# A SwiGLU feed-forward whose gate-and-up product is cut into halves: eight products of halves against seven

## The chip, the core and the metric

One core of a Trainium2 chip runs the whole program. The metric is the device time of one execution in microseconds (us). Five engines take part: TensorE (PE in the profile, with its weight loads as PEld), VectorE (DVE), ScalarE (ACT), GpSimd (POOL) and SyncE (SP), which here only issues transfers.

## The reference, cut to what matters

The program computes two layers of a decoder trunk on 512 tokens of 1024 features. Each layer adds to the residual `x` a first feed-forward, a token mixer (pooling, attention, a state-space branch called S5) and a second feed-forward, each read through an RMS norm that is scaled and shifted by vectors made from a conditioning vector `c` (the reference calls this adaLN):

```python
mod = (jax.nn.silu(c) @ ada_w + ada_b).reshape(B, N_MOD, D_MODEL)   # nine vectors per layer
h = _modulate(_rms_norm(x, norm_ffn1), sh1, sc1)
x = x + 0.5 * g1[:, None, :] * _swiglu(h, ffn1_w_in, ffn1_w_out)

def _swiglu(h, w_in, w_out):              # w_in (1024, 5632), w_out (2816, 1024)
    gate, up = jnp.split(h @ w_in, 2, axis=-1)
    return (jax.nn.silu(gate) * up) @ w_out
```

Everything is float32.

## The kernel before, in words

**Names.** A feed-forward is called by layer and place: (0,1), (0,2), (1,1), (1,2). Its 2816 hidden features are 22 blocks `f` of 128. The 22 are worked through in `CHUNKS` of 6, 6, 6 and 4.

**Matmuls.** A float32 operand is kept as two parts, `hi` (rounded to the type fp32r, by ScalarE) and `lo` (the rest, by VectorE). `mm3` makes one product of three matmuls: hi by hi, hi by lo, lo by hi. For one block `f`, `glu_mm` does 8 slices of 128 features, gate and up, three matmuls each: 48 matmuls of 512 columns (one for each token). `glu_post` then applies SiLU, multiplies gate and up and splits the result. After a chunk its blocks are multiplied by `w_out` and `x_update` (VectorE, L417) adds them to `x`: for a chunk of 6 that is 144 matmuls of 512 columns. In the last chunk, of 4 blocks, `out_halves` does this for each half of the tokens apart, in 192 matmuls of 256 columns, so that the norm of the next stage (`norm_half`) can begin with the finished half. The first two blocks of a feed-forward are likewise done in halves of 256 columns as the norm delivers them, feature slice by feature slice (all but the very first feed-forward).

**Weights.** They come as one stream of units of 512 KB in the order of `stream_plan`. `loader` fetches a unit into one of two raw buffers, `splitter` makes its `hi` (ScalarE, L404, 128x1024) and `lo` (VectorE, L413, 128x1024) into one of four slots of each kind, and the matmuls that have used a unit give its slots back (`done`). Gate and up take two units per block `f`, `w_out` one unit per block.

**Other work beside the matmuls.** `ada_task` streams `ada_w` in pieces of 512 KB and multiplies each by SiLU(c) on VectorE (L417, 128x1024): seven vectors of layer 0 (56 pieces) in the feed-forward (0,1), nine vectors of layer 1 (72 pieces) in (0,2). `s5_build` prepares tables for the mixer, in (0,1) and in (1,1), much of it on GpSimd (L440).

**The order of the work.** There is no hand-written order. The kernel runs a small event simulation in the host program (`Sched`), with a cost for each instruction, and issues each instruction on its engine in the order in which the simulation reaches it. On the chip each engine keeps that order and waits on semaphores. So a costed order is fixed before the run, and an engine that is later than the simulation thought holds up what is queued behind it.

**Lines of helpers.** Every operation goes through a helper, so the profile names these lines: L404 ScalarE, L413 and L417 VectorE (two tensors; two tensors and a scalar), L440 GpSimd (two tensors), L453 matmul, L469 transpose, L546 DMA issue on SP.

Of the kernel before, what the change touches and what calls it, by code (L numbers as in the profile page):

```python
# [89 lines left out]

def wide_block(l, w):

    return FIRST_BLOCK if (l, w) == (0, 1) else 2


def stream_plan():

    plan = []
    for l in range(DEPTH):
        for w in (1, 2):  # L100
            if w == 2:
                for k4 in range(2):
                    plan += [("cv", l, k4), ("ka", l, k4)]
# [9 lines left out]
            f0 = 0  # L113
            for n in CHUNKS:
# [16 lines left out]
def pack_stream(inp):  # L131
# [240 lines left out]
def kernel(ctx, tc, xT, c, ada, ws, sp, mp, bc, w1, c_cols, ada_pe, cst, out):  # L372
# [79 lines left out]
    def mm(o, l, r, start=True, stop=True):  # L452
        nc.tensor.matmul(o, l, r, start=start, stop=stop)  # L453
# [80 lines left out]
    raws = Slots(K, ["r0", "r1"])  # L534
# [16 lines left out]
    def loader():  # L551
        for i, u in enumerate(plan):
# [3 lines left out]
            rn = yield from raws.get()  # L556
            r = sbt([128, 1024], F32, rn)
# [3 lines left out]

    def splitter():
        for i, u in enumerate(plan):
            yield dmax[i]
            d = units[i]
            n = unit_cols(u)
            hn = yield from his.get()
            hi = sbt([128, 1024], F32R, hn)[:, :n]
            t = pts(hi, d["raw"], 1.0, 1.0) if u[0] in POOL_HI else act(hi, d["raw"])
            ln = yield from los.get()  # L570
            lo = sbt([128, 1024], F32R, ln)[:, :n]
            yield t
            t = (ptt if i in POOL_LO or u[0] in POOL_LOK else tt)(lo, d["raw"], f(hi), OP.subtract)
            raws.put(d["rn"], t)
            d.update(hn=hn, ln=ln, hi=hi, lo=lo)
            K.set(d["ev"], t)
# [22 lines left out]
    def ada_task(l, ms, slots, scr, pace, after):  # L599
# [14 lines left out]
        for i, (m, j) in enumerate(todo):  # L614
# [5 lines left out]
            t = stt(scr, slots[:, i % depth, :], 1.0, silu_c["c"], OP.mult, OP.mult,  # L620
# [85 lines left out]


# [109 lines left out]
    def out_halves(ufo, ah, al, aev, gcol, nxt, Rs):  # L817
# [7 lines left out]
        for half in nxt["order"]:  # L825
            for dg in range(2):
                wide = Rs is None and half == nxt["order"][0] and dg == 0
                for dis in ((0, 1, 2, 3),) if wide else ((0,), (1,), (2,), (3,)):
# [18 lines left out]
    def final_store(st):  # L847
        for half in range(2):
# [160 lines left out]
    def mixer(l, st, nxt, s5):  # L1009
# [734 lines left out]
        def attention():  # L1744
# [10 lines left out]
            yield all_p  # L1755
            K.set(nxt["gate"])
# [236 lines left out]
    def main():  # L1993
# [11 lines left out]
        for l in range(DEPTH):  # L2005
            s5 = dict(ev=Ev(), rot_ev=Ev(), room=Ev())
            K.spawn(s5_rot(s5))
            if l > 0:
                s5.update(alloc_s5())
                Kreg = sbt([128, 4096], F32, "K")  # L2010
                Vreg = sbt([128, 2048], F32, "V")
# [8 lines left out]
            else:  # L2020
                K.spawn(s5_build(l, s5, Kreg, Vreg))
            nx = new_norm(l, 1)
            for half in range(2):
                K.spawn(norm_half(nx, half))
            yield from ffn(l, 1, st, nx, s5["room"])
# [9 lines left out]
            if l + 1 < DEPTH:  # L2035
                Kreg = sbt([128, 4096], F32, "K")
                Qreg = sbt([128, 4, D], F32, "Q")
                K.spawn(ada_task1(Qreg, Kreg))
                nx = new_norm(l + 1, 0)
                for half in range(2):  # L2040
                    K.spawn(norm_half(nx, half))
            else:
                nx = new_norm(l, 0)
                K.spawn(final_store(nx))
            yield from ffn(l, 2, st, nx)
# [6 lines left out]
    def ada_task0(Qreg, Kreg):  # L2052
# [3 lines left out]
        yield from ada_task(0, [2, 3, 4, 5, 6, 7, 8], Qreg, scr, 2500, mod_ev)  # L2056
        K.set(ada_done[0])

    def ada_task1(Qreg, Kreg):
        yield K.now + 30000  # L2060
        yield from load_c(Kreg)
        yield from ada_task(1, list(range(9)), Qreg, Kreg[:, 1024:2048], 2500, mod_ev)
# [52 lines left out]
```

## Time and profile before

| what | us |
|---|---|
| median of 3 runs | 2084.37 |
| lowest and highest run | 2080.19, 2084.98 |
| the profiled execution: its time | 2086.14 |
| the profiled execution: span from first to last instruction | 2084.3 |
| busy in the span: TensorE | 2030.9 |
| VectorE | 1222.0 |
| ScalarE | 722.3 |
| GpSimd | 555.0 |

The profiled execution took 1.8 us more than the span of its instructions and also 1.8 us more than the median of the runs. A busy share is an average over stages that have different limits; what a change in a stage is worth is read from that stage.

### The profile page before, as it was taken

The page shows a single profiled execution, that of the slowest core. Times are in us where ns is not written, and L with a number is a line of the kernel's source. Part 1 is how long each engine was busy: PE and PEld are TensorE (multiplying, and loading weights), DVE is VectorE, ACT ScalarE, POOL GpSimd, SP SyncE. Part 2 cuts the span into 40 slices and gives each one's busy share as a digit, 9 for nine tenths or more (in the row PEclk, how much of TensorE's full clock was granted, in tenths as well). Part 3 has the DMA queues.
Part 4 walks back from the last instruction along what each step waited for, and adds up shares of the span by engine and source line. Part 5 has one row for each costly group of instructions (what it writes and reads, how often), then busy time and mean ns, then how long its engine had stood idle before and what let it go on. Part 6 is the DMA issues. An engine that isn't in the chain of part 4 may idle for free.

```text
span 2084.3 us, 27503 instructions
## 1 busy us (share of the span) xinstructions
PE 2030.9 (97%) x10538; PEld 1710.6 (82%) x10538; DVE 1222.0 (59%) x2165; ACT 722.3 (35%) x1262; POOL 555.0 (27%) x813
## 2 busy tenths in 40 slices
PE   5999999999999999999999999999999999999999
PEld 4788888897988888888898888889888888888888
DVE  6779743477876777774364334336678774333333
ACT  4423222343665522222242222224237644222221
POOL 4039102545735200000024400063466360000000
PEclk9999999999999999999999999999999999999999
DMA  6668722231200387773323222222211012222222
GB/s 244 250 212 286 247 91 92 79 111 49 67 21 22 117 276 254 262 263 130 97 86 111 91 91 91 91 91 101 81 44 61 1 61 101 91 92 98 95 91 82
DMA packets 71124, 251.34 MB, mean 121 GB/s; under 512 B 8016, under 2 KB 10448, under 8 KB 70480
## 3 DMA queue, kind: packets, MB, share of 16 engines
q1 hardware_dynamic: 70992, 249.58, 35.6%
q8 instruction: 83, 1.36, 0.3%
q14 instruction: 49, 0.40, 0.1%
HBM read 247.45 MB, written 2.10 MB: 120 GB/s over the span
## 4 chain that ended last, share of the span: by engine, by line
PE 85%; DVE 7%; POOL 3%; ACT 2%; issue 2%; DMA 0%; SPq 0%; DVEq 0%; POOLq 0%; ACTq 0%
PE p L453 83%; DVE s L413 3%; POOL s L440 3%; PE p L469 3%; DVE s L417 2%; ACT s L404 2%; DVE s L1274 1%; DVE s L422 0%; DVE p L1567 0%; DMA s<-in_x_dram 0%; DVE s L432 0%; POOL s L449 0%; ACT L404 0%; DVE s L1567 0%; DVE s L424 0%
## 5 line engine op out<-in xcount | busy, mean ns | idle before, releaser
L453 PE MATMUL p<-s,s 128*128 128x512 f32 (+5 forms) x9862 | 1978.2, 360 | 41.8 <-DVE s L413 21.1
L453 PEld LDWEIGHTS p<-s,s 128*128 128x128 f32 (+1 forms) x9862 | 1635.0, 193 | 348.7 <-DVE s L413 23.4
L413 DVE TENSOR_TENSOR s<-s,s 128x1024 fp32r<-128x1024 f32 (+7 forms) x558 | 516.7, 947 | 460.6 <-ACT s L404 450.2
L404 ACT ACTIVATE s<-s 128x1024 fp32r<-128x1024 f32 (+4 forms) x576 | 451.4, 806 | 756.5 <-PE p L453 587.9
L440 POOL TENSOR_TENSOR s<-s,s 128x256 f32<-128x256 f32 (+13 forms) x363 | 287.4, 811 | 242.7 <-DVE s L424 116.5
L404 ACT ACTIVATE s<-p 128x512 f32<-128x512 f32 (+9 forms) x325 | 162.8, 524 | 477.6 <-PE p L453 398.0
L440 POOL TENSOR_TENSOR s<-s 128x256 f32<-128x256 f32 (+4 forms) x244 | 165.3, 683 | 545.7 <-ACT s L404 402.7
L413 DVE TENSOR_TENSOR s<-s,p 128x512 f32<-128x512 f32 x89 | 60.9, 686 | 217.9 <-PE p L453 206.0
L417 DVE SCALAR_TENSOR_TENSOR s<-s,s 128x1024 f32<-128x1024 f32 (+1 forms) x143 | 182.0, 1276 | 1.8 <-DMA s<-in_ada_dram 0.3
L417 DVE SCALAR_TENSOR_TENSOR s<-p,s,s 128x512 f32<-128x512 f32 (+2 forms) x210 | 128.8, 620 | 68.6 <-PE p L453 67.4
L413 DVE TENSOR_TENSOR s<-p,s 128x512 fp32r<-128x512 f32 (+8 forms) x205 | 109.7, 556 | 52.4 <-ACT s L404 38.5
L469 PE MATMUL p<-s,s 128*128 128x128 f32 (+1 forms) x548 | 82.5, 278 | 8.2 <-DVE s L413 7.4
L469 PEld LDWEIGHTS p<-s,s 128*128 128x128 f32 (+1 forms) x548 | 66.6, 142 | 21.1 <-DVE s L413 7.7
L404 ACT ACTIVATE s<-p,s 128x512 f32<-128x512 f32 (+3 forms) x132 | 69.5, 533 | 30.1 <-DVE s L1567 22.3
L449 POOL TENSOR_SCALAR s<-s,s 128x512 f32<-128x512 f32 (+3 forms) x128 | 68.9, 560 | 24.1 <-DVE s L413 22.9
L449 POOL TENSOR_SCALAR s<-s 128x128 f32<-128x128 f32 (+9 forms) x58 | 34.0, 604 | 136.7 <-PE p L453 113.8
L1567 DVE CUSTOM_DVE_ANT_0 p<-p,s 128x512 f32<-128x512 f32 (+3 forms) x128 | 61.3, 500 | 9.7 <-PE p L453 9.5
L1809 POOL MEMSET s<- 128x8 f32 x2 | 0.2, 111 | 213.6 <-PE p L453 213.6
L404 ACT ACTIVATE s<-s,s 128x256 fp32r<-128x256 f32 x80 | 40.1, 507 | 47.1 <-DVE s L417 47.0
L417 DVE SCALAR_TENSOR_TENSOR s<-s,s,s 128x256 fp32r<-128x256 f32 (+2 forms) x100 | 49.1, 502 | 1.7 <-ACT s L404 1.5
L417 DVE SCALAR_TENSOR_TENSOR s<-s,s,p 128x256 f32<-128x256 f32 (+1 forms) x88 | 43.3, 502 | 6.8 <-PE p L453 5.2
L404 ACT ACTIVATION_READ_ACCUMULATOR s<-p,s 128x1 f32 x128 | 26.0, 203 | 0.0
(36 smaller groups left out, 204.2 us busy)
## 6 DMA issues: line engine op xcount, KB each, us to landing
s<-in_ws_dram SPq DMA_DIRECT2D x304, 512.0 KB, 3.5
s<-in_ada_dram SPq DMA_DIRECT2D x143, 512.0 KB, 5.2
s<-in_w_dram SPq DMA_DIRECT2D x4, 1024.0 KB, 6.3
s<-in_x_dram SPq DMA_DIRECT2D x8, 256.0 KB, 6.2
out_dram<-s SPq DMA_DIRECT2D x16, 128.0 KB, 1.7
s<-in_ws_dram SPq DMA_DIRECT2D x4, 420.0 KB, 3.2
s<-in_c_dram SPq DMA_DIRECT2D x2, 512.0 KB, 5.1
s<-in_bc_dram SPq DMA_DIRECT2D x2, 512.0 KB, 5.7
```

The costliest lines, as they stand in the source:

```text
L404: nc.scalar.activation(o, i, func, **kw)
L413: nc.vector.tensor_tensor(o, a, b, op)
L417: nc.vector.scalar_tensor_tensor(o, a, s, b, op0=op0, op1=op1, **kw)
L440: nc.gpsimd.tensor_tensor(o, a, b, op)
L449: nc.gpsimd.tensor_scalar(o, a, s1, s2, op0=op0, op1=op1)
L453: nc.tensor.matmul(o, l, r, start=start, stop=stop)
L469: nc.tensor.transpose(o, i, idn)
L1274: nc.vector.tensor_tensor_scan(zz, keep[:, 2, 4 * q + j:4 * q + j + 1].to_broadcast([128, 128]), zz, 0.0, op0=OP.mult, op1=OP.add)
L1567: nc.vector.tensor_tensor_reduce(b[:, :L], b[:, :L], mask, -0.125, 3.0e38, OP.add, OP.min, nmax[:, r:r + 1])
L1809: nc.gpsimd.memset(cosT[:, :, 0:1], 1.0)
```

## The change

In (0,2), (1,1) and (1,2) the blocks `f` are taken in pairs `j`. The weights of a pair are four quarter units, "11", "12", "21", "22" (block 1 or 2 of the pair, features 0 to 511 or 512 to 1023), still 512 KB each. The tokens are two halves of 256. Pair 0 is done with the ordinary eight products of a quarter by a half operand. Each of the other ten pairs takes seven products (Winograd's form of Strassen's scheme): "11" by b11, "12" by b21, "22" by t4, "s2" by m6, "s1" by n1, "s3" by m7, "s4" by b22. One product of a weight form by an operand is 2 (gate, up) x 4 (feature slices) x 3 matmuls of 256 columns, so 24. The forms s1 to s4 are sums of quarters, made in place in the raw buffers by two VectorE and two GpSimd additions of 128x1024 per pair; all seven forms are then split into `hi` and `lo`. The operands t4, m6, n1, m7 are sums of quarters of the normed activations, made once per feed-forward by `norm_ops`, beside b11, b21, b12, b22. The outputs are put together from PSUM by ScalarE copies (`snap`) and VectorE additions, and SiLU and the split (`finish`) run per half block of 256 columns.

The core of the diff:

```diff
+STR = {(0, 2), (1, 1), (1, 2)}
+LEAD, REST, LAST = ("11", "12"), ("22", "s2", "s1", "s3"), ("s4",)
+PLAIN = ("11", "12", "21", "22")
+def pair_groups():
...
+    out = [(1, LEAD), (2, LEAD[:1]), (0, PLAIN), (1, REST), (2, LEAD[1:]), (1, LAST)]
+    for j in range(2, NF // 2):
+        out.append((j, REST))
+        if j not in ends:
+            out.append((j + 1, LEAD))
+        out.append((j, LAST))
...
-    raws = Slots(K, ["r0", "r1"])
+    raws = Slots(K, ["r0", "r1", "r2", "r3"])
...
+    def splitter_pairs(l, w, js, skip):
...
+            yield dmax[idx[j, "21"]]
+            t3 = tt(blk("11"), blk("11"), blk("21"), OP.add)
+            yield dmax[idx[j, "22"]]
+            t1 = ptt(blk("21"), blk("21"), blk("22"), OP.add)
+            t = yield from made("22", blk("22"))
+            yield max(t, t3)
+            t2 = tt(blk("22"), blk("22"), blk("11"), OP.add)
+            yield t2
+            t = yield from made("s2", blk("22"))
+            sums[j] = t4 = ptt(blk("12"), blk("12"), blk("22"), OP.add)
...
+    def norm_ops(st, half, pb, bn, tn):
...
+        if first:
+            for k in range(8):
+                t = scaled(k)
+                yield t
+                K.spawn(put("b11" if k < 4 else "b21", k % 4, q[:, k], sh[:, k:k + 1]))
...
+            t2 = stt(d[:, 0:256], q1[:, k], sh[:, k:k + 1], q[:, 4 + k], OP.add, OP.add)
+            t3 = ptt(q[:, k], q1[:, k], q[:, k], OP.subtract)
+            yield t2
+            t4 = stt(q1[:, 4 + k], q1[:, 4 + k], sh[:, 4 + k:5 + k], d[:, 0:256], OP.add, OP.subtract)
+            K.spawn(put("n1", k, q[:, k], at=t3, pool=True))
+            K.spawn(put("m6", k, d[:, 0:256], sign=-1.0, at=t2, free=tn_))
+            K.spawn(put("m7", k, q[:, 4 + k], at=te, pool=True))
+            yield from put("t4", k, q1[:, 4 + k], sign=-1.0, at=t4)
...
+            te = stt(q[:, 4 + k], q[:, 4 + k], dsh[:, k:k + 1], q[:, k], OP.add, OP.subtract)
...
+    def ffn_pairs(l, w, st, nxt, room):
...
+        def prod(b, j, name, op, start, keep=False):
+            d = form(l, w, j, name)
+            yield d["ev"]
+            for part in range(2):
+                for k in range(4):
...
+                    t = mm3(b[:, part * 256:part * 256 + 256], d["hi"][:, cc], d["lo"][:, cc], o[:, k], o[:, 4 + k],
+                            start and part == 0 and k == 0, part == 1 and k == 3, skip_group_check=True)
...
+        def rest(j, A, f2, aev):
+            D = yield from bank()
+            t_d = yield from prod(D[1], j, "22", "t4", True)
+            t = yield from prod(A[1], j, "s2", "m6", False)
...
+            K.spawn(snap(A[1], t, u2))
+            C_ = yield from bank()
+            t_c = yield from prod(C_[1], j, "s1", "n1", True)
+            yield u2["ev"]
+            t = yield from prod(A[1], j, "s3", "m7", False)
+            K.spawn(snap(A[1], t, u3))
...
+                t1 = tt(y, C_[1], u3["s"], OP.add)
+                K.set(c22, t1)
...
+        def last_form(j, part, f2, aev):
...
+            yield c22
+            t = yield from prod(C_[1], j, "s4", "b22", False)
...
+            if ci == 0:
+                yield from start(1)
+                ahead[2] = yield from bank()
+                c1 = yield from lead1(2, ahead[2])
+                yield from plain_pair(aev)
+                part = yield from rest(1, ahead[1], 2, aev)
+                yield from lead2(2, c1, 4, aev)
+                yield from last_form(1, part, 2, aev)
...
+                        if dg == 0 and fp == 1:
+                            yield from hook()
```

Around it:

```diff
-                K.spawn(s5_build(l, s5, Kreg, Vreg))
+                def build1(s5=s5, Kreg=Kreg, st=st):
+                    yield st["ops_done"]
+                    yield st["plain_done"]
+                    yield kraw[l, 1]["ret"]
+                    s5.update(alloc_s5())
+                    yield from s5_build(l, s5, Kreg, sbt([128, 2048], F32, "V"))
...
-            nx = new_norm(l, 1)
+            nx = new_norm(l, 1, (0, 1) if l == 0 else (1, 0))
...
-                nx = new_norm(l + 1, 0)
+                nx = new_norm(l + 1, 0, (1, 0))
+                nx["gate"] = ada_done[1]
...
+        yield from ada_task(1, [0, 1, 2, 3, 4], [Qreg[:, i, :] for i in range(4)], scr, 2500, mod_ev)
         K.set(ada_done[0])
...
-        yield from ada_task(1, list(range(9)), Qreg, Kreg[:, 1024:2048], 2500, mod_ev)
+        slots = [Vreg[:, 0:1024], Vreg[:, 1024:2048]]
+        yield from ada_task(1, [5, 6, 7, 8], slots, None, 4000, mod_ev)
...
-    nc = _bacc.Bacc("TRN2", target_bir_lowering=False, num_devices=1)
+    nc = _bacc.Bacc("TRN2", target_bir_lowering=False, num_devices=1, dynamic_dma_scratch_size=512)
```

So 40 of layer 1's 72 `ada_w` pieces move into (0,1) and 32 stay in (0,2), there with two buffers instead of four. The S5 tables of layer 1 are begun later, when the operands and pair 0 are done. Raw buffers grow to four, and four more (the K area; two of them only at first in (1,1)) hold the quarters "21" and "22". The second half of the tokens goes first in the stages between. The scratch area for DMA descriptors is made smaller by the last line above.

## Rows read from the trace of the kernel before

**Rows 1.** The page's first part: span, then busy time by engine.

```profile
span 2084.3 us, 27503 instructions
PE 2030.9 (97%) x10538; PEld 1710.6 (82%) x10538; DVE 1222.0 (59%) x2165; ACT 722.3 (35%) x1262; POOL 555.0 (27%) x813
```

**Rows 2.** The chain that ended last: shares of the span by engine.

```profile
PE 85%; DVE 7%; POOL 3%; ACT 2%; issue 2%; DMA 0%; SPq 0%; DVEq 0%; POOLq 0%; ACTq 0%
```

**Rows 3.** Instruction groups by form, TensorE, whole span (busy us, mean ns, idle before).

```profile
L453 PE MATMUL p<-s,s 128*128 128x512 f32 x6210 | 1506.4, 400 | 14.5 <-ACT s L404 7.6 <-DVE s L413 5.7 <-POOL s L440 1.1
L453 PE MATMUL p<-s,s 128*128 128x256 f32 x2780 | 379.7, 294 | 10.4 <-DVE s L417 4.6 <-ACT s L404 3.1 <-DVE s L422 2.3
```

**Rows 4.** VectorE timeline, end of (0,2): start us, length us, operation.

```profile
1004.26 0.69 DVE L413 TENSOR_TENSOR s<-s,p 128x512 f32<-128x512 f32 x1 [3.59 <-PE p L453]
...
1037.86 0.69 DVE L413 TENSOR_TENSOR s<-s,p 128x512 f32<-128x512 f32 x1 [3.54 <-PE p L453]
...
1046.24 0.48 DVE L417 SCALAR_TENSOR_TENSOR s<-p,s,s 128x256 f32<-128x256 f32 x1 [0.93 <-PE p L453]
...
1050.46 0.48 DVE L417 SCALAR_TENSOR_TENSOR s<-p,s,s 128x256 f32<-128x256 f32 x1 [0.93 <-PE p L453]
```

**Rows 5.** Windows: us, busy by engine (instructions), clock, DMA share, GB/s.

```profile
100.00:140.00 40.00, 40.00 (x172) 32.18 (x171) 28.19 (x83) 8.80 (x11) 4.97 (x5) 1.00 0.62 214
140.00:180.00 40.00, 40.00 (x173) 32.07 (x172) 39.79 (x48) 10.40 (x12) 38.74 (x29) 1.00 0.78 263
1040.00:1050.00 10.00, 10.00 (x87) 10.00 (x87) 4.11 (x9) 2.88 (x7) 3.68 (x5) 1.00 0.16 52
```

**Rows 6.** Instruction groups by form, whole span, VectorE, ScalarE, GpSimd.

```profile
L417 DVE SCALAR_TENSOR_TENSOR s<-p,s,s 128x512 f32<-128x512 f32 x112 | 83.2, 747 | 21.7 <-PE p L453 20.8
L413 DVE TENSOR_TENSOR s<-s,p 128x512 f32<-128x512 f32 x89 | 60.9, 686 | 217.9 <-PE p L453 206.0 <-ACT s L404 7.1 <-PE p L469 4.8
L413 DVE TENSOR_TENSOR s<-s,s 128x256 fp32r<-128x256 f32 x32 | 13.7, 447 | 7.3 <-ACT s L404 7.3
L404 ACT ACTIVATE s<-s 128x1024 fp32r<-128x1024 f32 x300 | 317.2, 1059 | 636.9 <-PE p L453 587.9 <-DMA s<-in_ws_dram 32.0 <-DVE s L417 9.1
L404 ACT ACTIVATE s<-p 128x512 f32<-128x512 f32 x109 | 66.2, 617 | 330.8 <-PE p L453 320.1 <-PE p L469 10.3
L440 POOL TENSOR_TENSOR s<-s,s 128x1024 f32<-128x1024 f32 x3 | 8.3, 2761 | 8.2 <-DMA s<-in_ada_dram 8.2
```

**Rows 7.** The same query by stretch: 750 to 910 us, then 140 to 220 us.

```profile
L413 DVE TENSOR_TENSOR s<-s,s 128x1024 fp32r<-128x1024 f32 x29 | 35.5, 1224 | 30.5 <-ACT s L404 30.4
...
L413 DVE TENSOR_TENSOR s<-s,s 128x1024 fp32r<-128x1024 f32 x16 | 24.6, 1540 | 1.3 <-ACT s L404 1.3
```

**Rows 8.** VectorE timeline, the norm between (0,2) and (1,1).

```profile
1064.61 0.48 DVE L417 SCALAR_TENSOR_TENSOR s<-s,s,s 128x256 fp32r<-128x256 f32 x1
...
1069.55 0.48 DVE L417 SCALAR_TENSOR_TENSOR s<-s,s,s 128x256 fp32r<-128x256 f32 x1
...
1078.08 0.48 DVE L417 SCALAR_TENSOR_TENSOR s<-s,s,s 128x256 fp32r<-128x256 f32 x1 [0.18 <-ACT s L404]
```

**Rows 9.** TensorE timeline at the start of (0,2), with the idle time before each piece.

```profile
683.55 3.30 PE L453 MATMUL p<-s,s 128*128 128x256 f32 x21 [0.71 <-DVE s L422]
687.41 3.09 PE L453 MATMUL p<-s,s 128*128 128x256 f32 x24 [0.56 <-DVE s L417]
691.26 1.63 PE L453 MATMUL p<-s,s 128*128 128x256 f32 x12 [0.76 <-DVE s L417]
693.72 66.67 PE L453 MATMUL p<-s,s 128*128 128x256 f32 x366 [0.83 <-DVE s L417]
```

**Rows 10.** VectorE timeline there: the last operand slice of the first half.

```profile
696.79 0.48 DVE L417 SCALAR_TENSOR_TENSOR s<-s,s,s 128x256 fp32r<-128x256 f32 x1
```

**Rows 11.** VectorE by form, 60 to 240 us: the `ada_w` pieces of layer 0.

```profile
L417 DVE SCALAR_TENSOR_TENSOR s<-s,s 128x1024 f32<-128x1024 f32 x50 | 68.8, 1376 | 0.5
```

**Rows 12.** TensorE timeline: the first transpose of the mixer of layer 0.

```profile
441.53 0.66 PE L469 MATMUL p<-s,s 128*128 128x128 f32 x4 [0.27 <-ACT s L404]
```

More of the change, by code (lines that the diff above doesn't have):

```diff
@@ L113, in stream_plan @@
             f0 = 0
+            if (l, w) in STR:
+                groups = pair_groups()
+                for n in CHUNKS:
+                    while groups and groups[0][0] < (f0 + n) // 2:
+                        j, forms = groups.pop(0)
+                        if forms is not LAST:
+                            plan += [("ga", l, (w, j, b)) for b in (("21", "22") if forms is REST else forms)]
+                    for dg in range(2):
+                        for f in range(f0, f0 + n, 2):
+                            plan.append(("fo", l, (w, f, dg)))
+                    f0 += n
+                assert not groups
+                continue
             for n in CHUNKS:
@@ L555, in loader @@
                 yield wgate[i]
-            rn = yield from raws.get()
-            r = sbt([128, 1024], F32, rn)
+            if u[0] == "ga" and (u[2][2][0] == "2" or u[2][1] == 0):
+                key = (u[1], u[2][0])
+                yield kraw[key]["ev"]
+                pool = kraw[key]["slots"]
+                rn = yield from pool.get()
+                r = kraw[key]["tile"][:, rn * 1024:(rn + 1) * 1024]
+                units[i]["pool"] = pool
+            else:
+                rn = yield from raws.get()
+                r = sbt([128, 1024], F32, rn)
+                units[i]["pool"] = raws
             units[i].update(rn=rn, raw=r[:, :n])
@@ L560, in loader, with open_kraw, split @@
             yield K.now
+    forms = {}
+    def open_kraw(l, w, ktile, n):
+        kraw[l, w].update(tile=ktile, slots=Slots(K, [0, 1, 2, 3]), n=n, gone=0, ret=Ev())
+        K.set(kraw[l, w]["ev"])
+    def split(src):
+        hn = yield from his.get()
+        hi = sbt([128, 1024], F32R, hn)
+        t = act(hi, src)
+        ln = yield from los.get()
+        lo = sbt([128, 1024], F32R, ln)
+        yield t
+        t = tt(lo, src, f(hi), OP.subtract)
+        return dict(hn=hn, ln=ln, hi=hi, lo=lo), t
@@ new lines, in plain @@
+    def plain(i):
+        u, d = plan[i], units[i]
+        yield dmax[i]
+        n = unit_cols(u)
+        hn = yield from his.get()
+        hi = sbt([128, 1024], F32R, hn)[:, :n]
+        t = pts(hi, d["raw"], 1.0, 1.0) if u[0] in POOL_HI else act(hi, d["raw"])
+        ln = yield from los.get()
+        lo = sbt([128, 1024], F32R, ln)[:, :n]
+        yield t
+        t = (ptt if i in POOL_LO or u[0] in POOL_LOK else tt)(lo, d["raw"], f(hi), OP.subtract)
+        d["pool"].put(d["rn"], t)
+        d.update(hn=hn, ln=ln, hi=hi, lo=lo)
+        K.set(d["ev"], t)
@@ L562, in splitter @@
     def splitter():
+        skip = set()
         for i, u in enumerate(plan):
[L564 to L573, printed above, removed]
@@ L574, in splitter @@
-            raws.put(d["rn"], t)
-            d.update(hn=hn, ln=ln, hi=hi, lo=lo)
-            K.set(d["ev"], t)
+            if u[0] == "ga":
+                if i not in skip:
+                    js, e = [], i
+                    while e < len(plan) and plan[e][0] == "ga":
+                        js.append(plan[e][2][1])
+                        skip.add(e)
+                        e += 1
+                    yield from splitter_pairs(u[1], u[2][0], set(js), skip)
+            elif i not in skip:
+                yield from plain(i)
@@ L652, in new_norm @@
                   xev=[[Ev() for _ in range(8)] for _ in range(2)])
+        if (l, 2 if idx == 2 else 1) in STR and idx != 1:
+            names = ("b11", "b21", "b12", "b22", "m6", "m7", "n1", "t4")
+            st.update(ops={}, oev={n: [Ev() for _ in range(4)] for n in names}, ops_done=Ev(), plain_done=Ev())
         return st
@@ L683, in norm_half @@
             yield st["gate"]
+        if "ops" in st:
+            yield from norm_ops(st, half, pb, bn, tn)
+            return
         if "h" not in st:
@@ L847, in final_store @@
     def final_store(st):
-        for half in range(2):
+        for half in st["order"]:
             lo, hi = HALVES[half]
```

349 lines of the change are left out of this document (324 added, 25 removed).

## The prediction

> **What bounds the kernel now.** I read the page's totals first: TensorE is busy 2030.9 of 2084.3 us, VectorE 59% [rows 1]. The chain that ended last says the same from the other side: 85% of it is TensorE, 7% VectorE [rows 2]. So time is saved by giving TensorE less to do, as long as nothing else runs late. The third view, forms on one engine, shows how TensorE's time is spent: 6210 matmuls of 512 columns and 2780 of 256 [rows 3]. Their "mean ns" overlap each other and must not be added up. The rate has to be read elsewhere.
>
> The clean rate is in the distance between events that each stand for a fixed number of matmuls. In (0,2), VectorE's first step after a block `f` comes at 1004.26 and, three blocks later, at 1037.86 [rows 4]: 11.20 us per block of 48 matmuls, so 233.3 ns for 512 columns. In `out_halves` the updates of `x` come at 1046.24 and, three outputs of 12 matmuls later, at 1050.46: 1.407 us each, so 117.2 ns for 256 columns. Twice 117.2 is 234.4, so cutting a matmul in half costs almost nothing (1 ns), though the weight loads then fill their track, 10.00 of 10 us [rows 5].
>
> **The change, part by part.**
>
> *Gate and up.* A pair took 2 x 48 x 233.3 ns = 22.40 us. With seven products it is 7 x 24 x 117.2 ns = 19.69 us. That is 2.71 us less per pair, and with 10 pairs in each of three feed-forwards 81.3 us less. Pair 0 is 192 matmuls of 256 columns before and after: nothing. The `w_out` matmuls are the same: nothing. Weight traffic is four units of 512 KB per pair before and after: nothing, with the raw buffers for 11 and 12 loaded one pair ahead; without that cover each load would show.
>
> *What VectorE gets for it.* Per pair 7 splits and 2 sums of 128x1024, at 1.22 us [rows 7]: 11.0. Four additions from PSUM at 0.69 [rows 6]: 2.7. Eight small steps of 128x256 at about 0.45 [rows 6]: 3.6. Together 17.3 us against TensorE's 19.69. A whole chunk of 6 blocks is 3 x 19.69 + 144 x 0.2333 = 92.7 us of TensorE and 3 x 17.3 + 6 x 1.22 + 8 x 0.75 = 65 us of VectorE: the `w_out` stretch gives it time to recover. ScalarE has 7 x 1.06 + 3 x 0.62 and eight steps of about 0.4 [rows 6], 12.5 us: no bound. GpSimd gets two sums of up to 2.76 us [rows 6].
>
> GpSimd and VectorE disturb each other. From 100 to 140 us VectorE is busy 28.19 us with GpSimd nearly idle, from 140 to 180 us 39.79 with GpSimd at 38.74 [rows 5], and a split goes from 1224 to 1540 ns [rows 7]. The trace has no long GpSimd sum beside splits. Its cost to VectorE per pair is at least nothing, at most the sums' whole length, 5.5 us. So a pair costs VectorE 17.3 to 22.8 us. TensorE is ahead of it up to 19.69. I take the low end, since GpSimd runs only 5.5 of 19.7 us, and price it below. The Trainium skill, "SBUF — State Buffer", section "SBUF: two physically separate sides", has a rule on this: the port pair shared by VectorE and GpSimd is an exclusive lock for a whole instruction, taken by a VectorE step with two SBUF inputs against a GpSimd step that reads SBUF. The longer VectorE times beside GpSimd agree with it; by that rule the high end would hold, which is the second case below.
>
> *New waits.* s3 writes the bank that ScalarE copies out after s2. Between them is the product of s1, 2.8 us, and the copy takes 0.62 [rows 6]. s4 waits (`c22`) for a copy and an addition, 0.62 + 0.69 and the hand-overs; between are the two leading products of the next pair, 5.6 us, or `w_out` matmuls; only 2.8 us in pair 1 and in the last pair of a feed-forward. Behind a late addition stand s4, then all of TensorE. Three feed-forwards x 1 us: +3.
>
> *Start of a feed-forward.* Before, TensorE began with two blocks at once and used one feature slice per 12 matmuls, 1.4 us, as the norm delivered them. Now the first product wants slices 0 to 3 and the second 4 to 7, after only 24 matmuls each. At (1,1), slice 3 is there at 1065.1 and slice 7 at 1070.0 [rows 8]. TensorE is through with `out_halves` eight outputs after 1050.46, less the last step's own delay: at about 1060.1 (1050.46 + 7 x 1.407 = 1060.3) [rows 4]. The second product can end at 1070.1 + 0.35 + 1.4 = 1071.9 and holds 5.6 us of work: 6.2 us idle that were none before. At (0,2), TensorE is ready at 686.85, slice 7 is there at 697.3 [rows 9, 10]: the same reckoning gives 6.7 us idle, of which 2.15 were idle before (0.56 + 0.76 + 0.83 [rows 9]): 4.6 us. I take 4.6 for (1,2), whose norm also follows a mixer. Sum 15.4.
>
> The operands of sums come next. At (1,1) the second half's plain slices were done at 1078.6 [rows 8]; the new forms in between push that to some 1082. The sums add 20 VectorE steps of 0.45 (9 us) and 12 on GpSimd; so 1091 at the earliest, 1097 with disturbance. They are wanted when the first-half work (19.7 us) and the second-half part of pair 0 (11.2) are done: 1060.1 + 6.2 + 30.9 = 1097.2. They are just covered. For this I put 1.5 us each, 0 to 5. Start of three feed-forwards: 15.4 + 4.5, about +20.
>
> *Moved work.* In (0,1), 40 more `ada_w` pieces: 50 took the 180 us from 60 to 240 [rows 11], 3.6 us each, so they end near 390 us, and the mixer begins at 441 [rows 12]. Covered; if not, the mixer waits. TensorE lost nothing there with VectorE at 39.79 of 40 [rows 5]. In (0,2), 32 pieces x 1.38 us [rows 11] = 44 us fall in chunks with 27 us to spare each; the simulation places them in VectorE's gaps, but it knows no disturbance. Between 0 and 44 x 59 / 92.7 = 28 us (the share of gate and up); I take 4. SP takes those transfers between weight units with two buffers instead of four; a late piece would hold the weights queued behind it, and four raw buffers cover that. In (1,1) the S5 tables' GpSimd work now meets the sums: some 45 splits made 0.32 us longer [rows 7] are 14 us at most, against VectorE's spare time; I take 4. The start of the program has two more raw buffers: nothing either way, bounded by some 2 us.
>
> **The sum.** Own time 2086.1 - 81.3 + 20 + 3 + 4 + 4 = 2035.8. The profiled execution lay 1.8 us above the median of the runs, so as a median 2034 us.
>
> **The rivals.**
>
> *Case 1, as summed,* 2034 us; its own range is 2017 to 2052, with the small costs each at either end.
>
> *Case 2, VectorE and GpSimd in turn set the pace* of gate and up. If two thirds of the sums' 5.5 us fall on VectorE, a pair takes it 17.3 + 3.7 = 21.0 us, 1.3 above TensorE. The last pair of a chunk can run late into the `w_out` stretch, so 20 pairs pay: 26 us, 2060. For it: the swing from 28 to 40 us [rows 5]. Against it: the sums are short beside the pair, and VectorE has 27 us to spare in a chunk.
>
> *Case 3, the other side:* the same mechanism with all of the 5.5 us and no relief from `w_out`. The pair then takes 22.8 us on VectorE, 0.4 more than TensorE needed before, so 30 x 0.4 = 12 us are lost instead of 81 gained: 2084 + 12 + 31 (the other terms) = 2127. It is slower than before from the point where a pair takes over 22.40 - 31 / 30 = 21.4 us. Against it: it needs every sum to stand in VectorE's way for its whole length.
>
> *Case 4, the starts are hidden:* the simulation puts the norm's steps ahead of everything, VectorE gets slices out every 0.9 us, and the +20 shrinks to 5 and the small terms to 2: 2084.3 - 81.3 + 7 = 2010.
>
> **Chances and range.** Case 1 0.62, case 2 0.20, case 3 0.05, case 4 0.13. The measurement tells 0.3%, some 6 us, from no change. Faster by more: all but case 3 and the worst of case 2, 0.92; within: 0.03; slower: 0.05. Range 2009 to 2066: it holds case 1, most of case 4 and the lower half of case 2.
>
> **What would show it.** Matmuls of 256 columns rise by 30 x 168 = 5040, those of 512 fall by 2880, and a pair inside a chunk takes 19.7 us. Each of the three feed-forwards opens with 5 to 8 us of TensorE idle, released by VectorE. The prediction is wrong if pairs take 20.5 us or more with TensorE waiting for L413 in mid-chunk (case 2 or 3), if the mixer of layer 0 starts late, or if 256 columns do not keep 117 ns when every matmul is so.

## The result and the profile after

The changed kernel took 2095.13 us (median of 4 runs, 2089.43 to 2099.31), the kernel before in the same comparison 2082.56 (4 runs): a ratio of 1.0058, 95% interval 1.003 to 1.0087. So it is slower, by 12.6 us, where 50 us of gain were forecast, and it lies above the whole range. The execution whose profile is read here is the shortest of the four, 2089.43 us at a mean granted clock of 0.982; the other three had 0.976 to 0.978. So the profiles lie closer together (3.3 us) than the medians.

The page's first part for the changed kernel, to be laid beside [rows 1]:

```profile
span 2087.5 us, 32821 instructions
PE 1976.0 (95%) x12698; PEld 1775.7 (85%) x12698; DVE 1608.0 (77%) x2630; ACT 895.3 (43%) x1622; POOL 782.4 (37%) x909
```

TensorE has less to do: 1976.0 us against 2030.9, 54.9 less. But its idle time, span less busy, went from 53.4 to 111.5, 58.1 more. The difference is the 3.2 us by which the span grew. The next view, TensorE's forms (busy, mean ns, idle before and who ended it), answers to [rows 3]:

```profile
L498 PE MATMUL p<-s,s 128*128 128x256 f32 x7820 | 1005.8, 289 | 66.5 <-DVE s L458 24.1 <-ACT s L449 23.0 <-DVE s L462 10.5
L498 PE MATMUL p<-s,s 128*128 128x512 f32 x3330 | 831.9, 404 | 12.2 <-DVE s L458 5.6 <-ACT s L449 5.3 <-POOL s L485 1.1
```

The counts are those forecast: 5040 more matmuls of 256 columns, 2880 fewer of 512. The idle time before the first form is 66.5 us, ended by VectorE (L458, L462) or by ScalarE's `hi` (L449). Windows show where it lies (columns as in [rows 5]): the openings of (0,2), (1,1) and (1,2) are 680 to 760, 1050 to 1130 and 1710 to 1790, the rest of (1,1) is 1130 to 1460, most of the rest of (1,2) 1790 to 2030; below them stand three short stretches.

```profile
680.00:760.00 80.00, 70.02 (x540) 67.55 (x539) 73.63 (x109) 42.98 (x80) 31.17 (x27) 0.94 0.19 66
1050.00:1130.00 80.00, 72.19 (x567) 69.32 (x567) 74.64 (x112) 43.50 (x81) 25.68 (x21) 0.98 0.22 74
1130.00:1460.00 330.00, 305.44 (x2090) 283.17 (x2089) 239.84 (x327) 130.25 (x201) 159.69 (x183) 0.96 0.27 95
1710.00:1790.00 80.00, 69.47 (x540) 66.93 (x539) 73.57 (x111) 43.51 (x83) 35.71 (x32) 0.94 0.15 48
1790.00:2030.00 240.00, 237.01 (x1587) 215.87 (x1586) 165.99 (x189) 99.99 (x143) 33.87 (x14) 1.00 0.31 106
...
690.00:700.00 10.00, 7.34 (x37) 6.79 (x37) 7.22 (x17) 3.71 (x8) 2.92 (x2) 0.67 0.28 100
1190.00:1200.00 10.00, 6.39 (x54) 5.98 (x53) 4.16 (x6) 2.50 (x5) 9.61 (x12) 1.00 0.01 2
1200.00:1210.00 10.00, 7.30 (x46) 6.89 (x46) 10.00 (x9) 3.68 (x6) 9.77 (x9) 0.83 0.35 110
```

Three things are to be seen. Behind the openings, in (1,2), TensorE loses 3.0 of 240 us. In the openings VectorE is busy 73.6 to 74.6 of 80 us and TensorE is idle 7.8 to 10.5 us in each. In (1,1) behind its opening TensorE is idle 24.6 us, much of it where the S5 tables keep GpSimd at 9.6 to 9.8 of 10 us. There VectorE is not always full: in the second of the short stretches it is busy 4.16 of 10 us (below). And where TensorE has waited, the granted clock falls: 0.67 and 0.83 in two of these 10 us stretches mean that part of them ran at 1.2 instead of 2.4 GHz. That lengthens the busy time too, which is most of why the busy time fell by 54.9 us and not by the 81.3 that were forecast.

To compare kernels I count, in steps of 10 us, TensorE's idle time and (1 - granted clock) x length, and call the sum *lost time* (an upper count, since an idle moment can also be one of low clock). The kernel before loses 6.1 us in the three openings, 0.5 in the rest of (1,1), 3.4 in the rest of the other two. The changed one loses 40.2, 36.8 and 14.9: 81.9 more, as much as the whole gain of 81.3.

How a GpSimd sum holds VectorE can be seen one by one in (1,2). First VectorE's steps, then GpSimd's at the same time (start, length):

```profile
1870.11 2.78 DVE L458 TENSOR_TENSOR s<-s,s 128x1024 fp32r<-128x1024 f32 x1 [0.78 <-ACT s L449]
...
1874.14 1.22 DVE L458 TENSOR_TENSOR s<-s,s 128x1024 f32<-128x1024 f32 x1
1875.27 2.96 DVE L462 SCALAR_TENSOR_TENSOR s<-s 128x256 f32<-128x256 f32 x2
...
1892.99 0.41 DVE L462 SCALAR_TENSOR_TENSOR s<-s 128x256 f32<-128x256 f32 x1
```

```profile
1869.41 2.41 POOL L485 TENSOR_TENSOR s<-s 128x1024 f32<-128x1024 f32 x1 [11.86 <-DVE s L458]
1875.49 2.46 POOL L485 TENSOR_TENSOR s<-s,s 128x1024 f32<-128x1024 f32 x1 [3.67 <-ACT s L449]
```

The split at 1870.11 takes 2.78 us, the sum of the same size at 1874.14, with GpSimd idle, 1.22; the profile counts a held step as busy. The split ends 1.07 us after the GpSimd sum beside it (1872.89 against 1871.82), as if it had run only then. The two small steps at 1875.27 end 0.28 us after the second sum; one of this form with nothing beside it takes 0.41 us (1892.99). So a sum of 2.4 us holds VectorE for 1.6 to 2.1 us.

In (1,1) there is a second way, the reverse of the first: VectorE stands idle and waits for a GpSimd sum. VectorE's step at 1196.00, then GpSimd's at the same time:

```profile
1196.00 1.62 DVE L458 TENSOR_TENSOR s<-s,s 128x1024 f32<-128x1024 f32 x1 [5.84 <-POOL s L485]
```

```profile
1192.88 3.09 POOL L485 TENSOR_TENSOR s<-s 128x256 f32<-128x256 f32 x2
```

The second of these two GpSimd steps is a sum of a pair (1024 columns). It came late because S5 steps stood before it in GpSimd's order. VectorE's addition overwrites a quarter that this sum reads, so it had to wait, 5.84 us long. In (1,1) behind its opening VectorE's two-tensor steps (L458) wait 13.7 us for GpSimd's (L485) in all, against 3.1 without the two sums (e4 below). In the openings VectorE waits for GpSimd 0.8, 0.2 and 0.8 us: there it is held and does not wait.

### The profile page after: what moved, and what is told of

It reads as the page before. It is cut to its first block, busy times and chain, and to the rows that moved or that the text cites. A ratio compares the mean times of both kernels' runs of the same rounds, so it can differ in the third digit from the quotient of the medians.

```text
span 2087.5 us, 32821 instructions
## 1 busy us (share of the span) xinstructions
PE 1976.0 (95%) x12698; PEld 1775.7 (85%) x12698; DVE 1608.0 (77%) x2630; ACT 895.3 (43%) x1622; POOL 782.4 (37%) x909
## 5 line engine op out<-in xcount | busy, mean ns | idle before, releaser
L498 PE MATMUL p<-s,s 128*128 128x256 f32 (+5 forms) x12022 | 1923.6, 321 | 98.2 <-DVE s L458 46.0
L498 PEld LDWEIGHTS p<-s,s 128*128 128x128 f32 (+2 forms) x12022 | 1702.5, 194 | 287.1 <-DVE s L458 56.6
L458 DVE TENSOR_TENSOR s<-s,s 128x1024 fp32r<-128x1024 f32 (+8 forms) x774 | 764.8, 1012 | 280.5 <-ACT s L449 260.1
L449 ACT ACTIVATE s<-s 128x1024 fp32r<-128x1024 f32 (+4 forms) x900 | 614.4, 711 | 833.8 <-PE p L498 412.2
L485 POOL TENSOR_TENSOR s<-s 128x256 f32<-128x256 f32 (+7 forms) x274 | 260.3, 956 | 755.8 <-DVE s L458 613.0
L485 POOL TENSOR_TENSOR s<-s,s 128x256 f32<-128x256 f32 (+14 forms) x429 | 420.5, 1000 | 325.5 <-DVE s L469 116.5
L449 ACT ACTIVATE s<-p 128x512 f32<-128x512 f32 (+9 forms) x361 | 180.2, 521 | 257.9 <-PE p L498 189.6
L458 DVE TENSOR_TENSOR s<-p,s 128x512 f32<-128x512 f32 (+8 forms) x325 | 191.9, 604 | 64.8 <-ACT s L449 40.2
L462 DVE SCALAR_TENSOR_TENSOR s<-s,s 128x1024 f32<-128x1024 f32 (+3 forms) x179 | 211.9, 1191 | 6.0 <-DMA s<-in_ada_dram 4.7
L462 DVE SCALAR_TENSOR_TENSOR s<-p,s,s 128x512 f32<-128x512 f32 (+2 forms) x210 | 128.2, 619 | 52.7 <-PE p L498 49.5
L514 PEld LDWEIGHTS p<-s,s 128*128 128x128 f32 (+1 forms) x548 | 64.4, 141 | 20.9 <-DVE s L458 8.0
L449 ACT ACTIVATE s<-p,s 128x512 f32<-128x512 f32 (+3 forms) x132 | 69.4, 534 | 25.2 <-DVE s L2045 15.6
L494 POOL TENSOR_SCALAR s<-s,s 128x512 f32<-128x512 f32 (+3 forms) x128 | 66.2, 543 | 22.2 <-DVE s L458 15.1
L462 DVE SCALAR_TENSOR_TENSOR s<-s,s,s 128x256 fp32r<-128x256 f32 (+3 forms) x124 | 65.4, 548 | 0.6 <-ACT s L449 0.4
L462 DVE SCALAR_TENSOR_TENSOR s<-s 128x256 f32<-128x256 f32 (+3 forms) x72 | 56.8, 810 | 2.4 <-ACT s L449 1.6
L449 ACT ACTIVATE s<-s,s 128x256 fp32r<-128x256 f32 x80 | 38.7, 502 | 32.8 <-DVE s L462 32.7
L458 DVE TENSOR_TENSOR s<-s 128x256 f32<-128x256 f32 (+3 forms) x127 | 43.2, 353 | 11.8 <-POOL s L485 6.3
L462 DVE SCALAR_TENSOR_TENSOR s<-s,s,p 128x256 f32<-128x256 f32 (+1 forms) x88 | 41.9, 497 | 4.3 <-PE p L498 3.6
```

The source lines that it names most:

```text
L449: nc.scalar.activation(o, i, func, **kw)
L458: nc.vector.tensor_tensor(o, a, b, op)
L462: nc.vector.scalar_tensor_tensor(o, a, s, b, op0=op0, op1=op1, **kw)
L485: nc.gpsimd.tensor_tensor(o, a, b, op)
L494: nc.gpsimd.tensor_scalar(o, a, s1, s2, op0=op0, op1=op1)
L498: nc.tensor.matmul(o, l, r, start=start, stop=stop, **kw)
```

## The experiments

Theory A: GpSimd's work holds VectorE, and TensorE loses where VectorE has no room. Rivals: the sums are late as operands (somebody waits for them); the order of products at the opening is at fault; the S5 tables alone are. Each ratio is to runs of the kernel before beside it.

| kernel | median us | ratio, 95% interval | lost time: openings / rest of (1,1) / rest of (0,2), (1,2) |
|---|---|---|---|
| before | 2079.8 to 2083.1 | 1 | 6.1 / 0.5 / 3.4 |
| after | 2095.13 | 1.0058 (1.003, 1.0087) | 40.2 / 36.8 / 14.9 |
| e1_s5copy | 2076.55 | 0.9971 (0.9961, 0.9982) | 43.8 / 20.6 / 15.1 |
| e2_plain_first | 2085.5 | 1.0018 (1.0006, 1.003) | 39.0 / 29.1 / 15.0 |
| e3_sums_dve | 2040.9 | 0.9808 (0.9792, 0.9825) | 30.7 / 15.3 / 4.5 |
| e4_no_sums | 2031.39 | 0.9756 (0.974, 0.9773) | 29.3 / 9.5 / 3.5 |
| e5_idle_sums | 2092.61 | 1.004 (1.0026, 1.0054) | 58.1 / 26.5 / 11.1 |
| e6_both | 2043.56 | 0.9808 (0.9793, 0.9823) | 28.1 / 13.8 / 4.2 |
| e7_both_s5copy | 2029.52 | 0.9739 (0.9722, 0.9756) | 31.4 / 3.4 / 4.2 |
| e8_ops_dve | 2035.78 | 0.9772 (0.9749, 0.9795) | 22.9 / 13.8 / 4.9 |
| e9_sums_ops | 2048.35 | 0.9843 (0.9828, 0.9859) | 27.2 / 17.4 / 5.0 |
| e10_s5dve | 2032.18 | 0.9766 (0.9748, 0.9783) | 25.3 / 9.9 / 4.6 |
| e11_s5dve_old_order | 2043.78 | 0.9823 (0.9804, 0.9842) | 29.1 / 13.8 / 4.2 |
| e12_before_idle | 2093.12 | 1.0057 (1.0039, 1.0076) | 14.3 / 0.3 / 3.3 |

Openings are counted over 80 or 90 us from the start of each feed-forward, moved with the mixer before it. The parts that no experiment touches (the first feed-forward, the mixers) vary by up to 8 us between these profiles. The profiled execution was 4 to 8 us shorter than the median for after, e5, e9 and e11, and 6 longer for e7. So small differences of lost time say little.

**e1_s5copy**: the S5 tables of (1,1) not computed.

```diff
+            if l == 1:
+                act(or_, ar)
+                yield act(oi, ai)
+                return
             ptt(tA...
```

> Leaves out: the S5 tables B and A of layer 1 are filled by 16 ScalarE copies instead of being computed by 48 GpSimd steps (the later GpSimd steps of S5 stay). In the changed kernel, (1,1) loses 17.6 us of TensorE idle time and 8.6 us at half clock between 1170 and 1250 us. Theory (GpSimd's S5 steps hold up VectorE's splits and the sums queued behind them): most of that goes, 20 to 26 us faster than the changed kernel, about 2071. Rival (VectorE alone is too full in (1,1), whoever works beside it): 0 to 5 us faster, about 2092.

2076.55 us, 19 less than the changed kernel; the lost time fell only in the rest of (1,1), by 16.2. That is a little under the theory's 20 to 26. Of the 81.9 us that the changed kernel loses beyond the kernel before, 69.5 remain.

**e2_plain_first**: pair 0 goes first, taking a feature slice at a time, as the kernel before opened. The lines that set the order:

```diff
-PLAIN = ("11", "12", "21", "22")
+PLAIN = ("11", "21", "12", "22")
-    out = [(1, LEAD), (2, LEAD[:1]), (0, PLAIN), (1, REST), (2, LEAD[1:]), (1, LAST)]
+    out = [(0, PLAIN), (1, LEAD), (2, LEAD[:1]), (1, REST), (2, LEAD[1:]), (1, LAST)]
```

> Pair 0 is moved to the front of a feed-forward and done feature slice by feature slice, 12 matmuls a slice, as the first two blocks of the kernel before were; the leading products of pairs 1 and 2 follow it. Theory (the opening loses time because the first two products want slices 0 to 3 and 4 to 7 at once, and TensorE's clock falls to half in the waits): about 8 us of idle time and clock come back in each of three feed-forwards, and the waits before the second product of pair 1 shrink as its form gets a slot earlier: 20 to 30 us faster than the changed kernel, about 2070. Rival (the opening is bound by the sum operands, which are wanted at the same time in either order): the waits move to the first use of t4, 0 to 6 us faster.

2085.5 us, 10 less, but not by what it was made for: the openings lost 39.0 instead of 40.2, and the gain stands in (1,1), 29.1 instead of 36.8. Neither theory (20 to 30 us) nor rival (0 to 6) came out, but the wide first products are not why the openings are long. The edit also keeps pair 0's quarters in the ordinary raw buffers, so that the S5 tables no longer wait for the K area to be given back; whether this or the order moved (1,1) is not separated.

**e3_sums_dve**: the two GpSimd sums of a pair on VectorE.

```diff
-            t1 = ptt(blk("21"), blk("21"), blk("22"), OP.add)
+            t1 = tt(blk("21"), blk("21"), blk("22"), OP.add)
-            sums[j] = t4 = ptt(blk("12"), blk("12"), blk("22"), OP.add)
+            sums[j] = t4 = tt(blk("12"), blk("12"), blk("22"), OP.add)
```

> The two sums per pair that GpSimd makes are made by VectorE. Theory (a GpSimd sum keeps VectorE's split out for its whole 2.4 us, while on VectorE it costs 1.15): VectorE gains 2.5 us per pair, the waits of 0.3 to 1.1 us in mid-chunk go (about 12 us in the three feed-forwards), and in (1,1) the sums no longer queue behind S5's steps (another 5 to 10): 10 to 20 us faster. Rival (VectorE's own load is the limit): 2.3 us more per pair on VectorE, up to 30 us slower.

2040.9 us: 54 less, from two words, where 10 to 20 were expected: the openings and (1,1) gained too. Lost time fell in all three columns. This lies in the range of the prediction. Its page, to be read against that of the changed kernel:

```profile
span 2038.6 us, 32757 instructions
PE 1956.3 (96%) x12698; PEld 1762.4 (86%) x12698; DVE 1600.1 (78%) x2690; ACT 896.5 (44%) x1622; POOL 635.7 (31%) x849
```

VectorE has 60 instructions more and yet is busy 7.9 us less.

**e4_no_sums** leaves both sums out, so that s1 and s4 are split from unsummed quarters. **e5_idle_sums** is e4 with additions of constants on GpSimd where the sums stood, as many columns, which nobody reads.

```diff
-            t1 = ptt(blk("21"), blk("21"), blk("22"), OP.add)
+            t1 = K.now
+            K.spawn(idle_sum())      # e5 only: two additions of 512 columns; the same for t4
```

> Leaves out the two GpSimd sums per pair (the forms s1 and s4 are then split from unsummed quarters). Theory: the same gain as with the sums on VectorE and a little more, 12 to 24 us faster; what stays of the 82 us lost is the opening and S5. Rival (VectorE's own load): no change in mid-chunk, 0 to 4 us faster.

> The kernel without the two sums, plus, in their places, the same length of GpSimd work that nobody waits for: additions of constants, 2 x 512 columns, into a buffer that is not read. Leaves out the sums of s1 and s4 as before. Theory (GpSimd, while it works, keeps VectorE out of its steps with two operands in SBUF): the loss comes back although nothing depends on GpSimd, 2070 to 2095. Rival (what hurts is that s1 and s4 wait for a sum that takes 2.4 us and queues behind S5): it stays at 2031 to 2040.

2031.39 and 2092.61 us: the additions bring back 61 us though nobody waits for them. So lateness is not needed for the loss: GpSimd's work by itself makes one of this size. Of e4 the page's busy times, then the opening of (0,2):

```profile
PE 1954.7 (96%) x12698; PEld 1762.4 (87%) x12698; DVE 1531.5 (75%) x2630; ACT 897.9 (44%) x1622; POOL 629.9 (31%) x849
...
680.00:760.00 80.00, 72.64 (x577) 70.37 (x577) 69.78 (x114) 47.59 (x86) 24.71 (x27) 0.96 0.24 80
```

and of e5, with the opening of (1,2) too:

```profile
PE 1977.5 (95%) x12698; PEld 1780.6 (85%) x12698; DVE 1615.6 (78%) x2630; ACT 895.9 (43%) x1622; POOL 830.5 (40%) x969
...
680.00:760.00 80.00, 68.25 (x490) 65.66 (x489) 76.25 (x107) 40.17 (x77) 42.20 (x36) 0.87 0.14 47
1710.00:1790.00 80.00, 68.88 (x494) 66.46 (x495) 75.38 (x106) 40.91 (x77) 42.16 (x34) 0.87 0.17 53
```

The same 2630 VectorE instructions take 84.1 us more. In the opening VectorE goes from 69.78 to 76.25 of 80 us and the granted clock from 0.96 to 0.87. By lost time 28.8 of the difference stand in the openings, 17.0 in the rest of (1,1), 7.6 in the rest of the other two. The sums of the changed kernel kept GpSimd busy for some 156 us (60 of 2.6 us), these additions for 207, so e5 is about a third more than the same dose. And late sums do cost something in (1,1). There e5 loses 26.5 us with the larger dose, the changed kernel 36.8; and L458 waits 3.1 us for L485 there in e5, as in e4, against 13.7 in the changed kernel. From these two differences (10.3 and 10.6 us) I estimate the price of lateness at 10 us; no run isolates it.

From the same pages: the sums on GpSimd cost VectorE 1608.0 - 1531.5 = 76.5 us, on VectorE 1600.1 - 1531.5 = 68.6. Moving them off VectorE relieved it of nothing.

**e6_both** is e2 and e3 together; **e7_both_s5copy** is e6 with e1's edit (S5 tables of (1,1) not computed).

> Sums on VectorE and pair 0 first, slice by slice. Theory (two separate losses): in the kernel with the sums on VectorE each opening still has some 5 us of waits for operand slices and 4 to 5 us of half clock; with both, 15 to 20 us under 2041, about 2023. Rival (the waits only move to the first use of t4): the 10 us that the reordering alone gave, about 2031, or less.

> As the last one, but leaves out the S5 tables of layer 1 as in the first experiment. Theory (S5's GpSimd steps hold VectorE in (1,1) even with the sums gone: 8.4 us of idle time and 3.4 at half clock between 1155 and 1200 us): 8 to 12 us less than with both changes alone. Rival (S5 hurt only because sums queued behind it): 0 to 3 us less.

2043.56 us: no gain over e3, where theory said 15 to 20 us; here the new order brings nothing (in e8 and e9 it does). 2029.52 us: 14 less than e6, with (1,1) at 3.4 us of lost time. So the S5 tables cost time beside the splits even without sums on GpSimd.

**e8_ops_dve** is e6 with `norm_ops`' GpSimd steps on VectorE; **e9_sums_ops** is e8 with the changed kernel's opening order.

```diff
-            t3 = ptt(q[:, k], q1[:, k], q[:, k], OP.subtract)
+            t3 = tt(q[:, k], q1[:, k], q[:, k], OP.subtract)
-                t = (ptt if pool else tt)(o[:, 4 + k], src, f(o[:, k]), OP.subtract)
+                t = tt(o[:, 4 + k], src, f(o[:, k]), OP.subtract)
```

> Sums on VectorE, pair 0 first, and the 12 GpSimd steps per feed-forward that make the operands n1 and m7 on VectorE too. Theory: VectorE's operand steps take 0.96 us beside GpSimd instead of 0.48, so 12 more steps of 0.4 cost less than they free: 2 to 4 us less per opening, 6 to 12 in all. Rival (VectorE's load is the limit there): up to 5 us more per opening, 15 in all.

> Sums and the operand steps of n1 and m7 on VectorE, with the order of the changed kernel at the opening (leading products of pairs 1 and 2 before pair 0). Theory as it now stands (the opening is set by VectorE's operand work, and the order only moves the waits): the same as with pair 0 first, 2036 plus or minus 5. Rival (the order matters once VectorE is relieved of GpSimd): 8 us slower than that, 2044.

2035.78 us for e8, 7.8 less than e6, and the openings lose 22.9 instead of 28.1. Part of what is left there comes without GpSimd, as the stretch shows in which the opening of (0,2) of e8 loses most, with GpSimd at nothing and VectorE nearly full:

```profile
720.00:730.00 10.00, 6.46 (x47) 5.56 (x46) 9.42 (x17) 2.72 (x6) 0.00 (x0) 1.00 0.00 0
```

e9 took 2048.35: here the edit of e2 does matter, 12.6 us, as the rival had it (8) and not the theory (none). Its trace does not place that well: TensorE idles in the openings as long as in e8 (17.0 and 17.8 us), and most of what it loses beyond e8 is granted clock, 5.1 us more in the openings and as much in the mixers (means over the runs: 0.980 to 0.983, against 0.985 to 0.994). Why the clock was lower is open.

**e10_s5dve** is e8 with the S5 tables of (1,1) on VectorE (`ptt` to `tt` in `s5_build` for layer 1); **e11_s5dve_old_order** is e9 with the same.

> As the kernel with sums and operand steps on VectorE and pair 0 first, plus the 48 GpSimd steps that compute the S5 tables of layer 1 on VectorE. Theory (a GpSimd step of 256 columns keeps VectorE out for its 0.62 us and more; on VectorE it costs about 0.35): 48 x 0.3 = 14 us of VectorE time come back in (1,1), of which TensorE sees 5 to 10: about 2028. Rival (VectorE's load is the limit in (1,1)): 0 to 10 us slower, up to 2046.

> The same with the opening in the order of the changed kernel: all GpSimd work that the change set beside VectorE is then on VectorE, and nothing else is touched. Theory: 2028 plus or minus 6. Rival (load): up to 2046.

2032.18 and 2043.78 us. (1,1) loses 9.9 instead of 13.8, and 13.8 instead of 17.4; the times fell by 3.6 and 4.6, which the intervals do not tell from nothing. e11 missed its theory (2028 plus or minus 6); again the opening's edit makes the difference, 11.6 us. e10 computes all that the reference does and is the fastest such version here: 0.9766 of the kernel before, 48 us faster, not told apart from e8 (0.9772).

**e12_before_idle**: the kernel *before*, with two of e5's additions for every pair of blocks.

```diff
             if u[0] == "fi" and (u[1], u[2][0]) != (0, 1) and u[2][2] == 1:
+                K.spawn(idle_sum())      # twice 512 columns, per block
```

> The kernel before, with two GpSimd additions of constants per pair of chunks (66 in all, two times 512 columns each) in three of its four feed-forwards, which nobody reads. Theory: GpSimd's additions cost time only through VectorE, by holding its steps, and only where VectorE is full; in gate and up of the kernel before VectorE is less full than in the changed one (in the products of the pairs it has none of the splits of summed quarters and fewer folds), so the same additions cost 0 to 4 us, 2080 to 2086. Rival: the additions slow the chip wherever they stand (TensorE or its operands too), and cost the 61 us that they cost in the changed kernel: 2100 to 2145.

2093.12 us against 2081.39 beside it, 11.7 more: neither number. Its page, the openings of (0,2) and (1,2), the rest of (1,2), and 10 us of (1,1):

```profile
PE 2029.8 (97%) x10538; PEld 1706.5 (82%) x10538; DVE 1270.5 (61%) x2165; ACT 721.2 (35%) x1262; POOL 761.4 (36%) x945
...
680.00:760.00 80.00, 74.71 (x417) 64.03 (x418) 66.08 (x86) 31.89 (x47) 47.09 (x32) 1.00 0.53 185
1710.00:1790.00 80.00, 75.55 (x416) 64.43 (x415) 46.83 (x60) 29.89 (x45) 42.66 (x30) 1.00 0.28 93
1790.00:2030.00 240.00, 240.00 (x1029) 192.58 (x1028) 85.80 (x91) 57.38 (x67) 24.18 (x18) 1.00 0.29 94
1170.00:1180.00 10.00, 10.00 (x45) 8.01 (x43) 2.61 (x2) 1.74 (x3) 9.56 (x11) 1.00 0.37 107
```

The same GpSimd load (206 us more than before) cost 61 us in e5 and 12 here. Behind the openings it cost nothing: TensorE is busy 240.00 of 240 us beside 24.18 us of GpSimd. In the 10 us of (1,1) GpSimd is busy 9.56, as much as in the short stretches of the changed kernel above (9.61 and 9.77); here TensorE is busy throughout, with VectorE at 2.61. So GpSimd does not slow TensorE itself. My 0 to 4 us were too low: the openings of the kernel before lost 14.3 instead of 6.1 us. They too hang on VectorE: in the opening of (1,1) TensorE now waits 1.65 and 1.40 us for the norm's operand steps (L417), where the kernel before did not wait.

## Why the prediction was wrong

**Where the miss lies.** For the profiled execution the prediction had 2035.8 us; it took 2089.43, 53.6 more. Two terms make that up. Idle time was to rise by 20 + 3 + 4 + 4 = 31 us and rose by 58.1, so 27.1 too much. Busy time was to fall by 81.3 us and fell by 54.9, so 26.4 too little.

**TensorE's work: counts and rate right.** The counts came out to the matmul, and in (1,2) 168 matmuls of 256 columns, a whole pair, take 19.70 us, against the 19.69 forecast. That is TensorE's timeline of the changed kernel at full clock; below it stands a pair in mid-chunk of (0,2):

```profile
1866.04 19.70 PE L498 MATMUL p<-s,s 128*128 128x256 f32 x168 [0.71 <-ACT s L449]
1886.45 8.75 PE L498 MATMUL p<-s,s 128*128 128x256 f32 x49 [0.71 <-ACT s L449]
...
819.64 5.96 PE L498 MATMUL p<-s,s 128*128 128x256 f32 x50 [0.49 <-DVE s L458]
826.12 5.78 PE L498 MATMUL p<-s,s 128*128 128x256 f32 x46 [0.52 <-DVE s L458]
832.21 8.45 PE L498 MATMUL p<-s,s 128*128 128x256 f32 x72 [0.31 <-ACT s L449]
841.77 5.95 PE L498 MATMUL p<-s,s 128*128 128x256 f32 x50 [1.12 <-DVE s L458]
```

From start to start the first is 20.4 us, with 0.71 of waiting for an `hi`. The pair in (0,2) takes 22.1 us (819.64 to 841.77), with 1.95 us of waits, 1.64 of them for VectorE's L458 (the two-tensor helper, L413 in the kernel before). That is the sign that the prediction named for its cases 2 and 3. A second pair like it begins at 916.34. With the sums on VectorE (e3) the rest of (0,2) up to 1040 loses 0.8 us instead of 7.6.

**The step that failed: "I take the low end".** The cost of the sums to VectorE was bounded by 0 and 5.5 us per pair and taken as nothing. It was 76.5 / 30 = 2.55 us per pair, near the middle. With 17.3 + 2.55 = 19.9 us VectorE is level with TensorE's 19.69. The full 5.5 us, which the prediction drew from the rule that it quoted, and which are its case 3 and not the second case as it says, were not reached. The rule is that of the Trainium skill, "SBUF — State Buffer", section "SBUF: two separate sides": of two steps that want the shared port pair, the first has it for the whole instruction and "the other fully blocks". The trace agrees: the split at 1870.11 ended 1.07 us after the sum beside it.

**The place was wrong too, also in the rivals.** Cases 2 and 3 had the right mechanism but looked for it in mid-chunk, with TensorE waiting pair after pair. That part of the lost time grew by 11.5 us only (3 + 4 were allowed for `c22` and the `ada_w` pieces). The bulk fell in two other terms of the sum:

- *Start of a feed-forward, +20*: 34.1 us more lost time, of which 22.2 are idle time and 11.9 clock. The idle part is near the forecast only by luck: in e9, with the same order but without the sums and `norm_ops`' steps on GpSimd, it is 11.0. By lost time, e4 against the changed kernel says that 11 of the 40.2 us are the sums, e8 against e6 that some 5 more are `norm_ops`' own GpSimd steps. The disturbance had been put at 1.5 us for each opening.
- *S5 tables against the sums, +4*: 36.3 us, of which 24.3 are idle time and 12.0 clock. Without the tables (e1) 16 go, without the sums (e4) 27. Beyond the kernel before, the tables alone cost 9.0 (e4) and the sums alone 20.1 (e1), 29.1 in all, but 36.3 side by side: such prices cannot be added one by one. In the changed kernel GpSimd is busy 159.69 of the 330 us of (1,1) behind its opening. The term knew splits made longer; it did not know sums that queue behind S5 steps while VectorE stands idle.

**A term was missing: the granted clock.** The sum knew only idle time. Of the lost time 23.9 us are clock (5.1 + 1.7 + 5.1 in the openings, 12.0 in the rest of (1,1)); the kernel before has none in these stretches. Over the whole span it is 37.5 us against 20.4. These 17.1 us are some two thirds of the 26.4 by which the busy time fell too little; what the rest is stays open.

**The other steps.** The mixer of layer 0 begins at 443.99 instead of 441.53 [rows 12]: the moved `ada_w` pieces cost 2.5 us at most. Case 4, hidden starts, was far off: no full version here lost less than 22.9 us in the openings.

Shown by the runs: GpSimd's work costs the gain (e3, e4, e5), through VectorE and not through TensorE (e12), and most of that without anybody waiting for its results (e5). Read from the trace and not isolated by a run: that in (1,1) late sums cost some 10 us besides. Only argued: why VectorE's sums do so much less harm than GpSimd's at nearly the same busy time (1600.1 and 1608.0). The event simulation places a VectorE sum behind more urgent steps, whereas a GpSimd sum holds whichever VectorE step it meets, an urgent operand too. No run tested this by itself.

## What to carry to other kernels

Before moving elementwise work to GpSimd, price what it takes from VectorE: here two sums of 1024 columns cost VectorE more from GpSimd (2.55 us per pair) than done on VectorE itself (2.29). Look for the price where VectorE is already full, and where GpSimd has a queue of its own, not at the average: the same GpSimd load cost 61 us in a kernel with VectorE at 75% and 12 us in one at 59%. A change that takes matmuls away pays only if the engine that feeds them keeps room, so read the windows of each stage's opening and add the clock that scattered waits cost.

## What the runs showed of the hardware that was not expected

- A GpSimd sum held even small VectorE steps for most of its 2.4 us: two steps of 128x256 took 2.96 us together beside one, where one of the form alone takes 0.41.
- The price of the hold was not the same in the two kernels: additions of constants cost VectorE 84.1 / 60 = 1.4 us for each 1024 columns in e5 and 48.5 / 66 = 0.73 in e12, where VectorE was busy less of the time.
- Short waits went with a lower clock: in 690 to 700 of the changed kernel TensorE is idle for 2.66 us of 10 and the granted clock is 0.67, so part of that stretch ran at 1.2 GHz.
- Matmuls of 256 columns with a weight load each kept 117.3 ns over a whole pair (19.70 us for 168); behind the opening of (1,2) the weight loads are busy 215.87 of 240 us.
